# Moving score, inversion and fill work inside a chunked RWKV-7 recurrence

## The chip, the cores and the metric

One core of a Trainium2 chip runs the whole kernel in one launch. PE is the tensor engine, PEld its weight loads, DVE the vector engine, ACT the scalar engine, POOL GpSimd, SP the queue that issues the transfers. The metric is device time in microseconds (us), lower is better; a kernel's time is the median of its runs.

## The reference, cut to what matters

Two layers on 272 tokens (16 learned tokens and 256 of the sequence) of width 2048, all in float32: an RWKV-7 time mixer and an MLP, then gated linear attention and an MLP. The change touches the first mixer only:

```
def step(S, inp):                                   # for each of 32 heads of 64, token after token
    r_t, w_t, k_t, v_t, a_t, b_t = inp
    sa = einsum('bhvk,bhk->bhv', S, a_t)
    S = S * w_t + sa b_t^T + v_t k_t^T
    y = einsum('bhvk,bhk->bhv', S, r_t)
v = xv @ w_rkv[2]                                   # value product
out = ((groupnorm(y) + bonus) * g) @ w_o            # output product
```

## The kernel before

**Products.** Every large product is done as three matmuls of 128x128 weights against 272 tokens, with both operands split into a high and a low part. `wload` (L122) fetches a piece of 128x1024 weights (`raw`, three buffers, SP), rounds it to `hi` on ACT (L132) and subtracts to `lo` on DVE (L133); `hi` and `lo` have two buffers each. A piece serves eight products; `mm3` (L136) is one product, its matmuls have lines L138, L139 and L140. In the recurrence `hi` and `lo` are made in two halves each (`split_parts` = 2).

**The recurrence in chunks.** The 272 tokens are four chunks of 64 and one of 16; the 32 heads are four groups of eight (g = 0 to 3). Within a chunk the recurrence is a small triangular system:

- `scores(g, c)` (L403): PE multiplies keys (`BK`) and receptance and removal vectors (`AR`) of one chunk into two `pt` banks, DVE masks them into `AM` (`AMr` for the short chunk).
- `invert(g)` (L419): DVE alone inverts the triangles of all five chunks of a group. It is a generator of 52 steps: ten transposes into `sysA`, 30 steps of forward substitution (two instructions each, `upd` and `sysA`, each needs the one before it), twelve transposes back (L441 into `t11`, L445 into `AM`). It needs the masks of all chunks.
- `merge(g)` (L518): PE and ACT put the 32-row halves together, in two parts. Its first matmuls have line L530 and need L441's transposes.
- Then for each chunk, in order: `state` (L579: PE on the state `S`, line L587, then DVE `rs`, L590), `solve` (L593: PE L599, ACT `uv`), `emit` (L604: PE L611, DVE adds to and decays `S`, PE L619, ACT `yc`), `turn` (L624: back to `hres`), and `centre` (L548), `keys` (L561), `inner` (L569) for the chunk to come. `state` of a chunk needs `S` from `emit` of the chunk before.
- `norm(g)` (L635): the group norm and the gate, a generator of eight steps; its matmuls are L643 and L652, its DVE lines L647 and L653.

**Fill products.** `products` (L708) is a generator of single products: the value products (256), then the output products of the first twelve of 16 input blocks (192). `R(n)` runs n of them, `until(n)` runs on to the n-th, `some(it, n)` takes n steps of another generator. A value product of group g must be done before group g starts. `split(g)` (L659, ACT and DVE) makes high and low parts of the finished y of a group, which the output products read.

**What sets the order.** In the block from L745 PE's order is the written order. The other engines and the transfers are ordered by a planner at build time, by the order of writing (pieces of weights far ahead of it) and by its own estimate of when each instruction is ready. In group g the kernel runs, for each chunk: `state` and `turn`; a score call of the next group or a few fills; `solve`; `centre`, `keys`; a further score call; fills; `emit`; `inner`. `GAPS` holds the two numbers of fills of each chunk.

The key products (L448 to L478), one for each of 16 blocks f, come before the recurrence; each is 16 products and a string of DVE and ACT work on their result, with two small matmuls (L461, L476). The products write `pj` and `pt` banks in turn, two of each. In them stand the scores of group 0 (after f = 9) and inversion 0 (after f = 13).

## Time and profile before

| what | value |
|---|---|
| median of three runs | 2668.19 us (2666.27 to 2672.52) |
| the profiled execution, its own time | 2671.53 us |
| its span, first to last instruction | 2669.7 us |
| granted PE clock, mean | 0.981 |
| first L530 of merge 0, 1, 2, 3 | 328.2, 410.7, 499.3, 589.9 us |

How to read it: the page gives for each engine its busy time and the number of its instructions. A row of stretches gives begin and end and length, then for each engine its busy time and the count, the granted clock, the share of the DMA engines and GB/s. A row of waits has the engine and line that waited, the one it waited for, total us, times, and the longest. A row in order of time has start, duration, engine, line, operation, tiles written and read, shape and count; in brackets the idle time of the engine before it and who ended it. A row of groups ends with busy us, the mean ns of one, and the idle time before them.

### The profile page before, as it was taken

To read this page: it belongs to the slowest core of one execution; us is meant where nothing else is said; L and a number is where in the kernel's file an instruction comes from. 1 tells how busy PE (TensorE), PEld (TensorE's weight loads), DVE (VectorE), ACT (ScalarE), POOL (GpSimd) and SP (SyncE) were. 2 spreads that over 40 slices of the span, in tenths; PEclk is the share of its full clock that TensorE was granted. 3 is DMA by queue.
4 is the path that set the end of the run, shared out by engine and by line. 5 is a ranking of instruction groups with operands and counts; after the bars stand their busy time and mean duration, and the time that the engine had idled before them with its cause. 6 is when DMAs were issued, how large, how long until landed. Compare 5 with 4: busy or idle time off the path is not lost.

```text
span 2669.7 us, 47686 instructions
## 1 busy us (share of the span) xinstructions
PE 2553.1 (96%) x19492; PEld 2369.1 (89%) x19492; DVE 1687.8 (63%) x2794; ACT 1258.0 (47%) x2011; POOL 10.8 (0%) x35
## 2 busy tenths in 40 slices
PE   7999887779999999999999999999999999999998
PEld 7888886668999999999999999988888888888887
DVE  8678966674755545545545666776766656656665
ACT  5465543435554434434434544454555535435444
POOL 0000000000000000000000000000000000000000
PEclk9999988889999999999999999999999999999999
DMA  5567622213445555545555544444555555555554
GB/s 189 177 226 260 223 92 72 85 58 106 160 166 177 179 174 175 179 176 174 176 179 174 178 152 144 174 150 142 190 184 188 189 190 189 188 187 188 188 189 158
DMA packets 136026, 450.16 MB, mean 169 GB/s; under 512 B 14704, under 2 KB 22640, under 8 KB 135808
## 3 DMA queue, kind: packets, MB, share of 16 engines
q1 hardware_dynamic: 135808, 447.12, 48.4%
q8 instruction: 153, 2.51, 0.4%
q14 instruction: 65, 0.53, 0.1%
HBM read 431.07 MB, written 15.99 MB: 167 GB/s over the span
## 4 chain that ended last, share of the span: by engine, by line
PE 76%; DVE 1%; ACT 0%; issue 0%; DVEq 0%
PE pj L166 23%; PE pj L138 13%; PE pj L140 13%; PE pj L139 13%; PE pj L167 12%; PE pt L899 1%; DVE lo L133 0%; PE pu L908 0%; PE pm L652 0%; PE pt L888 0%; PE pu L910 0%; PE pu L909 0%; PE pm L845 0%; PE pm L643 0%; DVE hres L978 0%; DVE sg L927 0%
## 5 line engine op out<-in xcount | busy, mean ns | idle before, releaser
L133 DVE TENSOR_TENSOR lo<-raw,hi 128x1024 fp32r<-128x1024 f32 (+1 forms) x834 | 946.8, 1142 | 617.4 <-ACT hi L132 603.9
L132 ACT CAST hi<-raw 128x1024 fp32r<-128x1024 f32 (+1 forms) x834 | 813.4, 983 | 1098.5 <-PE pj L139 585.3
L138 PE MATMUL pj<-x,hi 128*128 128x272 f32 x2224 | 661.7, 298 | 6.6 <-ACT x L306 4.1
L140 PE MATMUL pj<-x,lo 128*128 128x272 f32 x2224 | 649.2, 292 | 0.0
L139 PE MATMUL pj<-x,hi 128*128 128x272 f32 x2224 | 647.3, 291 | 0.0
L166 PE MATMUL pj<-x,hi 128*128 128x512 f32 x1664 | 587.9, 397 | 0.6 <-DVE x L818 0.6
L167 PE MATMUL pj<-x,lo 128*128 128x256 f32 x1664 | 469.5, 282 | 1.3 <-DVE lo L133 1.3
L138 PEld LDWEIGHTS pj<-x,hi 128*128 128x128 f32 x2224 | 425.6, 191 | 15.3 <-ACT x L306 4.9
L139 PEld LDWEIGHTS pj<-x,hi 128*128 128x128 f32 x2224 | 428.1, 192 | 2.1
L140 PEld LDWEIGHTS pj<-x,lo 128*128 128x128 f32 x2224 | 424.9, 191 | 0.7
L166 PEld LDWEIGHTS pj<-x,hi 128*128 128x128 f32 x1664 | 313.5, 188 | 76.2 <-issue 2.9
L166 PE MATMUL pj<-h,hi 128*128 128x512 f32 x1024 | 358.5, 395 | 0.0
L167 PEld LDWEIGHTS pj<-x,lo 128*128 128x128 f32 x1664 | 315.0, 189 | 2.9 <-DVE lo L133 1.9
L138 PE MATMUL pj<-h,hi 128*128 128x272 f32 x1024 | 295.3, 288 | 0.0
L140 PE MATMUL pj<-h,lo 128*128 128x272 f32 x1024 | 294.4, 288 | 0.0
L139 PE MATMUL pj<-h,hi 128*128 128x272 f32 x1024 | 294.0, 287 | 0.0
L167 PE MATMUL pj<-h,lo 128*128 128x256 f32 x1024 | 288.9, 282 | 0.0
L166 PEld LDWEIGHTS pj<-h,hi 128*128 128x128 f32 x1024 | 192.7, 188 | 43.6
L167 PEld LDWEIGHTS pj<-h,lo 128*128 128x128 f32 x1024 | 194.3, 190 | 0.0
L139 PEld LDWEIGHTS pj<-h,hi 128*128 128x128 f32 x1024 | 194.1, 190 | 0.0
L138 PEld LDWEIGHTS pj<-h,hi 128*128 128x128 f32 x1024 | 193.2, 189 | 0.0
L140 PEld LDWEIGHTS pj<-h,lo 128*128 128x128 f32 x1024 | 192.4, 188 | 0.0
(246 smaller groups left out, 2213.9 us busy)
## 6 DMA issues: line engine op xcount, KB each, us to landing
raw<-mlp_w_d SPq DMA_DIRECT2D x512, 512.0 KB, 3.2
raw<-gla_in_d SPq DMA_DIRECT2D x98, 512.0 KB, 3.2
raw<-w_rkv_d SPq DMA_DIRECT2D x80, 512.0 KB, 3.4
raw<-gla_o_d SPq DMA_DIRECT2D x32, 512.0 KB, 3.2
raw<-w_r_d SPq DMA_DIRECT2D x16, 512.0 KB, 3.3
raw<-rw_oA_d SPq DMA_DIRECT2D x16, 512.0 KB, 3.2
raw<-rw_oB_d SPq DMA_DIRECT2D x16, 512.0 KB, 3.2
ard<-ar SPq DMA_DIRECT2D x16, 288.0 KB, 3.5
```

The lines of the kernel that those rows point to most:

```text
L132: nc.scalar.copy(hi[:, h], raw[:, h])
L133: nc.vector.tensor_tensor(out=lo[:, h], in0=raw[:, h], in1=hi[:, h].bitcast(F32), op=ALU.subtract)
L138: nc.tensor.matmul(out, hi[:, ws], xh, start=first, stop=False)
L139: nc.tensor.matmul(out, hi[:, ws], xl, start=False, stop=False)
L140: nc.tensor.matmul(out, lo[:, ws], xh, start=False, stop=last)
L166: nc.tensor.matmul(wide, hi[:, ws], x[kt][:, :, off : off + SEQ], start=kt == 0, stop=False)
L167: nc.tensor.matmul(ps[:, :SEQ], lo[:, ws], x[kt][:, 0, off : off + SEQ], start=False, stop=kt == nk - 1)
L899: nc.tensor.matmul(pa[:w, i * C : (i + 1) * C], KX[i][:, dt, s * P : s * P + w], Q[:, dt, i * C : (i + 1) * C], start=dt == 0, stop=dt == 1)
```

## The change

- **Scores.** The five score calls of the next group were one in chunk 0, two in chunk 1 and two in chunk 2; now two in chunk 0 and three in chunk 1. The inversion of the next group is started in chunk 1 instead of chunk 2.
- **Inversion steps.** Portions of nine (twice in each chunk from chunk 1's end on) instead of eight and six; all 52 are written by chunk 4's first portion instead of 36 with the rest behind `until`.
- **Fills.** `GAPS` moves fills from the last chunks to chunk 2 and spreads group 3's evenly. `MARK` replaces the fixed marks: at the merges of groups 1, 2, 3 the fills stand at 134, 214, 286 instead of 120, 184, 248. Around the second half of a merge there are 4, 2 and 4 fills instead of 8, 4 and 3. Groups 0 to 2 take 80, 80 and 72 fills instead of 64 each (the first of them with those that open the next group).
- **Inversion 0** runs in portions of seven in each key product after f = 7; the scores of group 0 come after f = 6 instead of 9, their loads after f = 4 instead of 7.
- **Weight pieces** come from one list (`order`, `srcs`); `ahead` asks for the next piece at the fourth product of the one that is running, instead of at its own first.
- **Norm steps** are taken four in each of chunks 0 and 1, instead of four, three and the rest.
- **Loads.** `AR` of the group after next is fetched in two parts, in chunks 3 and 4, instead of once behind the group; `BK` in chunk 2 as before.
- The last split and the last 64 output products join `order`; they run after `until(448)` and the release of the recurrence's memory, where they stood before.

```
-GAPS = [[(2, 1), (2, 1), (2, 1), (8, 8), (8, 8)],
-        [(2, 1), (2, 1), (2, 1), (8, 8), (8, 8)],
-        [(2, 1), (2, 1), (2, 2), (10, 10), (10, 10)],
-        [(2, 2), (2, 2), (10, 10), (10, 10), (10, 10)]]
+GAPS = [[(2, 1), (2, 1), (8, 8), (9, 9), (9, 9)],
+        [(2, 1), (2, 1), (8, 8), (9, 9), (9, 9)],
+        [(2, 1), (2, 1), (8, 8), (8, 8), (8, 8)],
+        [(4, 4), (4, 4), (4, 4), (4, 4), (4, 4)]]
+MARK = [134, 214, 286]
...
+        def fetch(g, dst, src, a=0, b=576):
+            nc.sync.dma_start(dst[g % 2][:, :, a:b], src[4 * g : 4 * g + 4, :, a:b].rearrange("f p n -> p f n"))
...
-            if f == 7:
+            if f == 4:
                 load(0)
-            if f == 9:
+            if f == 6:
                 for c in range(5):
                     scores(0, c)
-            if f == 13:
-                for _ in invert(0):
-                    pass
+                inv = invert(0)
+            if f > 7:
+                for _ in range(7):
+                    next(inv, None)
...
-                hi, lo = self.wload(s)
+                hi, lo = weights.pop(0)
                 for j in range(8):
+                    if j == 3:
+                        ahead()
...
+        def ahead():
+            if srcs:
+                weights.append(self.wload(srcs.pop(0)))
...
             for g in range(NG):
-                V = 64 * (g + 2) if g < 3 else 0
+                more = g + 1 < NG
                 for c in range(5):
                     if c:
                         state(g, c)
                         turn(g, c - 1)
-                    if g + 1 < NG and c in (1, 2):
-                        scores(g + 1, 2 * c - 1)
-                        R(1)
-                    else:
+                    if more and c < 2:
+                        scores(g + 1, 2 * c)
+                    elif not more:
                         some(last, 1)
-                        R(GAPS[g][c][0])
-                    some(inv, 6)
+                    R(GAPS[g][c][0])
+                    some(inv, 9)
                     solve(g, c)
                     if c in (1, 3):
                         centre(g, c + 1)
                     if c < 3:
                         keys(g, c + 1)
-                    if g + 1 < NG and c < 3:
-                        scores(g + 1, 2 * c)
-                        if c == 2:
-                            inv = invert(g + 1)
-                    some(last, 3)
+                    if more and c < 2:
+                        scores(g + 1, 2 * c + 1)
+                    some(last, 4)
                     R(GAPS[g][c][1])
-                    some(inv, 8)
+                    if more and c == 1:
+                        scores(g + 1, 4)
+                        inv = invert(g + 1)
+                    some(inv, 9)
                     emit(g, c)
                     if c < 4:
                         inner(g, c + 1)
-                    if c == 2 and g + 2 < NG:
-                        load(g + 2, ar=False)
-                some(last, 99)
-                if g + 2 < NG:
-                    load(g + 2, bk=False)
-                if g + 1 < NG:
-                    until(V - 8)
+                    if g + 2 < NG and c == 2:
+                        fetch(g + 2, BKs, bkd)
+                    if g + 2 < NG and c == 3:
+                        fetch(g + 2, ARs, ard, 0, 512)
+                    if g + 2 < NG and c == 4:
+                        fetch(g + 2, ARs, ard, 512)
+                if more:
+                    until(MARK[g])
                     some(inv, 99)
                     m = merge(g + 1)
                     next(m)
-                    until(V)
+                    R(4)
                     turn(g, 4)
-                    R(4)
+                    R(2)
                     next(m)
                     for f in (centre, keys, inner):
                         f(g + 1, 0)
-                    R(3)
+                    R(4)
...
         for _ in last:
             R(4)
-        R(999)
+        until(448)
         win.close()
         wl.close()
-        split(3)
-        for f in range(8):
-            for _ in outB(1, f):
-                pass
+        R(999)
```

More of the change, by code (lines that the diff above doesn't have):

```diff
@@ L396, in put, with load @@
             tt(dst[:, o + skip : o + 16], a[:, 4 * C + skip :], b[:, 4 * C + skip :])
-        def load(g, bk=True, ar=True):
-            for on, dst, src in ((bk, BKs, bkd), (ar, ARs, ard)):
-                if on:
-                    nc.sync.dma_start(dst[g % 2], src[4 * g : 4 * g + 4].rearrange("f p n -> p f n"))
+        def fetch(g, dst, src, a=0, b=576):
+            nc.sync.dma_start(dst[g % 2][:, :, a:b], src[4 * g : 4 * g + 4, :, a:b].rearrange("f p n -> p f n"))
+        def load(g):
+            fetch(g, BKs, bkd)
+            fetch(g, ARs, ard)
         def scores(g, c):
@@ L665, in rwkv, with units @@
         loc = [hres[:, f] if f < 12 else rr[f - 4] for f in range(KT)]
-        def units(x, srcs, ps):
-            for i, s in enumerate(srcs):
-                hi, lo = self.wload(s)
+        def units(x, n, ps):
+            for i in range(n):
+                hi, lo = weights.pop(0)
                 for j in range(8):
+                    if j == 3:
+                        ahead()
                     kt = 8 * i + j
-                    self.mm3(ps, hi, lo, slice(j * P, (j + 1) * P), x[kt][:, 0], x[kt][:, 1], kt == 0,
-                             kt == 8 * len(srcs) - 1)
-                    if kt < 8 * len(srcs) - 1:
+                    self.mm3(ps, hi, lo, slice(j * P, (j + 1) * P), x[kt][:, 0], x[kt][:, 1], kt == 0, kt == 8 * n - 1)
+                    if kt < 8 * n - 1:
                         yield
@@ L679, in v_proj @@
             ps = self.pj()[:, :T]
-            yield from units(xv, pair(wv, f), ps)
+            yield from units(xv, 2, ps)
             nc.scalar.copy(hres[:, f], ps)
@@ L686, in outA @@
             ps = self.pj()[:, :T]
-            yield from units(yo, [ap["rw_oA"][f]], ps)
+            yield from units(yo, 1, ps)
             xin = rr[f % 8] if f < 12 else loc[f]
@@ L693, in outB @@
         def outB(s, fp):
-            hi, lo = self.wload(ap["rw_oB"][s, fp])
+            hi, lo = weights.pop(0)
             pss = [self.pj()[:, :T] for _ in range(2)]
@@ L697, in outB @@
                 for j in range(4):
+                    if (i, j) == (0, 3):
+                        ahead()
                     y = yo[8 + 4 * s + j]
@@ L706, in outB @@
                 yield
-        def products():
-            for f in range(KT):
-                yield from v_proj(f)
-            split(0)
-            split(1)
-            for f in range(8):
-                yield from outA(f)
-            split(2)
-            for f in range(2):
-                yield from outB(0, f)
-            for f in range(8, 12):
-                yield from outA(f)
-            for f in range(2, 6):
-                yield from outB(0, f)
-            for f in range(12, 16):
-                yield from outA(f)
-            for f in range(6, 8):
-                yield from outB(0, f)
+        order = [(v_proj, f) for f in range(KT)] + [(split, 0), (split, 1)] + [(outA, f) for f in range(8)] + [(split, 2)]
+        order += [(outB, 0, 0), (outB, 0, 1)] + [(outA, f) for f in range(8, 12)] + [(outB, 0, f) for f in range(2, 6)]
+        order += [(outA, f) for f in range(12, 16)] + [(outB, 0, 6), (outB, 0, 7), (split, 3)]
+        order += [(outB, 1, f) for f in range(8)]
+        srcs = []
+        for k, *a in order:
+            srcs += pair(wv, a[0]) if k == v_proj else [ap["rw_oA"][a[0]]] if k == outA else [ap["rw_oB"][a[0], a[1]]] if k == outB else []
+        weights = []
+        def ahead():
+            if srcs:
+                weights.append(self.wload(srcs.pop(0)))
+        def products():
+            for k, *a in order:
+                if k == split:
+                    split(*a)
+                else:
+                    yield from k(*a)
         work = products()
@@ L744, in rwkv @@
         load(1)
+        ahead()
         with tc.manual_schedule(engines={mybir.EngineType.PE}):
@@ L804, in rwkv @@
             R(4)
-        R(999)
+        until(448)
         win.close()
         wl.close()
-        split(3)
-        for f in range(8):
-            for _ in outB(1, f):
-                pass
+        R(999)
         self.split_parts = 1
```

## The prediction

> **What bounds the kernel now.** I read the page first, then busy time by stretch, then the waits of PE, then the vector engine (DVE) and PE in order of time inside the recurrence. The page's first lines:

> ```profile
> span 2669.7 us, 47686 instructions
> ## 1 busy us (share of the span) xinstructions
> PE 2553.1 (96%) x19492; PEld 2369.1 (89%) x19492; DVE 1687.8 (63%) x2794; ACT 1258.0 (47%) x2011; POOL 10.8 (0%) x35
> ```

> PE is idle for 2669.7 - 2553.1 = 117 us. The stretches below are, in turn: key products up to score group 0; from there to merge 0; then for each of groups 0 to 2 a front part (merge to the masks of score chunk 3) and a back part (to the next merge); last, group 3. Then come the waits of PE in 320 to 690 us, and the first merge.

> ```profile
> core 0: us, PE busy (x) PEld busy (x) DVE busy (x) ACT busy (x) POOL busy (x), PEclk, DMA share, GB/s
> 196.00:241.00 45.00, 43.39 (x315) 41.03 (x314) 34.06 (x85) 30.02 (x57) 0.00 (x0) 1.00 0.91 304
> 241.00:328.10 87.10, 76.45 (x554) 71.23 (x552) 84.20 (x233) 46.27 (x91) 0.16 (x1) 0.96 0.63 216
> 328.10:363.20 35.10, 33.22 (x530) 29.44 (x530) 11.85 (x22) 14.66 (x34) 1.46 (x2) 0.81 0.17 61
> 363.20:410.60 47.40, 32.27 (x422) 29.84 (x418) 44.65 (x110) 15.86 (x35) 0.16 (x1) 0.85 0.37 128
> 410.60:452.50 41.90, 37.36 (x576) 31.95 (x576) 16.87 (x33) 19.85 (x47) 1.46 (x2) 0.93 0.15 47
> 452.50:499.20 46.70, 29.56 (x403) 26.93 (x401) 44.12 (x108) 14.72 (x33) 0.16 (x1) 0.85 0.36 125
> 499.20:541.10 41.90, 37.38 (x575) 31.99 (x575) 16.82 (x33) 19.85 (x47) 1.46 (x2) 0.93 0.15 46
> 541.10:589.90 48.80, 29.59 (x405) 27.07 (x402) 46.45 (x117) 17.08 (x41) 0.16 (x1) 0.83 0.21 72
> 589.90:678.10 88.20, 83.48 (x1076) 75.75 (x1077) 43.53 (x88) 47.04 (x106) 0.52 (x1) 0.96 0.29 96
> ```

> ```profile
> PE pt L530 <- DVE sysA L441: 47.9, 4, 14.9
> PE pu L587 <- DVE S L266: 12.9, 9, 3.2
> ```

> ```profile
> 328.16 1.92 PE L530 MATMUL pt<-sysA,AM 32*32 32x32 f32 x64 [8.02 <-DVE sysA L441]
> ```

> So fronts are PE's, with DVE 34 to 40% busy; backs are DVE's, 94 to 95% busy, and PE sits out 15 to 19 us of each. What PE waits for is the inversion: 47.9 us at the four merges, 8.02 at merge 0 and so 39.9 at the other three. What DVE does in the stretch from 241 us and in the back of group 0: the inversion (first two rows, the tile sysA), then, by the groups of that back, pieces of weights (`lo`, two halves each); below them, by tile (ns: shortest, median, longest), the small ones that the sums need.

> ```profile
> 241.00:328.10 87.10, 32.19 (x82) 0.96 0.63 216
> 363.20:410.60 47.40, 31.83 (x82) 0.85 0.37 128
> ```

> ```profile
> L133 DVE TENSOR_TENSOR lo<-raw,hi 128x512 fp32r<-128x512 f32 x14 | 9.0, 686 | 0.3 <-ACT hi L132 0.3
> ```

> ```profile
> L266 DVE TENSOR_TENSOR S<-pu,S x2: 425/425/425, 368.3 to 382.4; 128x256 f32<-128x256 f32 x2
> L266 DVE TENSOR_TENSOR S<-S,WC x2: 420/423/426, 369.4 to 383.0; 128x256 f32<-128x256 f32 x2
> ```

> ```profile
> L590 DVE SCALAR_TENSOR_TENSOR rs<-pu,rs x32: 412/418/428, 351.3 to 652.3; 64x256 f32<-64x256 f32 x24, 32x256 f32<-32x256 f32 x8
> ```

> ```profile
> L647 DVE SCALAR_TENSOR_TENSOR ysq<-hres,vecs,ysq x16: 496/501/505, 428.1 to 677.1; 128x272 f32<-128x272 f32 x16
> L266 DVE TENSOR_TENSOR r<-r,ysq x16: 432/441/443, 428.6 to 677.6; 128x272 f32<-128x272 f32 x16
> ```

> **The change, part by part.** No arithmetic is added or removed: PE, ACT and DVE do the same products, so time can only come from waits and from the clock. Fill products are 448 before the last 64 in both; they only change place.

> *Inversion 0 among the key products.* Its 82 DVE instructions (32.2 us), and before them the score masks of group 0, move three to five key products earlier. DVE is full from 241 us until merge 0 (84.2 of 87.1) but has 45.0 - 34.1 = 10.9 us free in 196 to 241. The masks (five pairs, the full ones 1.29 us by the rows at 357.10 and 441.88 below, so about 6 us) go into that room, and inversion steps may follow, so DVE should be through 6 to 9 us earlier. PE lost 8.02 us there. I take 6. Bounds: 0, if the key products' own DVE work, now behind seven steps in each product, holds PE as long; 10, if wait and half clock both go. Price if its cover goes: rival C.

> The clock after such a wait, PE alone in three stretches of 3 us (busy and count, granted clock; the first is a run of fill products in the recurrence, the second follows merge 1, the third an S wait of 2.57 us, whose row stands below):

> ```profile
> 378.40:381.40 3.00, 3.00 (x24) 1.00 0.03 5
> 412.60:415.60 3.00, 3.00 (x13) 0.50 0.01 3
> 461.10:464.10 3.00, 3.00 (x14) 0.50 0.01 3
> ```

> ```profile
> 459.90 0.24 PE L587 MATMUL pu<-S,AR 64*64 64x64 f32 x1 [2.57 <-DVE S L266]
> ```

> A fill product (three matmuls) is 3.00/8 = 0.375 us at full clock, about 0.67 at half. After merge 0, half clock costs 18 matmuls some 2 us. Whether a shortened wait keeps the clock lies between 0 and 2; the third row fell to 0.50 after only 2.6 us, so I take 1. [...]

> *Scores in chunks 0 and 1, the front.* The masks of score chunk 2 in groups 0 and 1 are now, with the PE groups of 416 to 506 us for score calls and norm:

> ```profile
> 357.10 1.29 DVE L266 TENSOR_TENSOR AM<-pt,cst 128x512 f32<-128x512 f32 x2 [2.71 <-PE pt L412]
> ```

> ```profile
> 441.88 1.29 DVE L266 TENSOR_TENSOR AM<-pt,cst 128x512 f32<-128x512 f32 x2 [2.71 <-PE pt L412]
> ```

> ```profile
> L412 PE MATMUL pt<-AR,BK 64*128 64x128 f32 (+1 forms) x80 | 6.3, 275 | 0.1
> L652 PE MATMUL pm<-gs,g 128*128 128x272 f32 x16 | 4.7, 419 | 1.2 <-ACT ysq L644 1.2
> ```

> Score chunk 3 takes the place that chunk 2 has now (masks over at 358.4 and 443.2), plus one more call on PE (6.3/5 = 1.3 us) and one more fill (0.4). Group 0's front then is 358.4 + 1.7 - 328.1 = 32.0 us instead of 35.1. In group 1, fills between merge and first emit go from 8+4+3 to 4+2+4, five fewer (1.9 us, and some 0.6 less at half clock): 443.2 + 1.7 - 2.5 - 410.6 = 31.8, say 32 instead of 41.9, since the second half of the norm and chunk 1's emit move behind the masks. Group 2 the same.

> *The backs.* An inversion is a chain that DVE must end before a merge, so a back lasts what DVE has in it. To 47.4, 46.7 and 48.8 us I add: fills, by GAPS and the marks 65, 65 and 57 (now 50, 43, 43), one piece of weights for eight, 2 x 0.686 with 0.08 of overlap = 1.29: 10.5, 10.5 and 9.2 us against 9.0, 7.7 and 7.7; one value add (0.4); chunk 1's S pair (0.85) and chunk 2's two rs (0.84); in groups 1 and 2 four norm steps more, six DVE operations of 0.44 to 0.50 (the third kind, L653, taken as L647), less one that is there: 2.4. Backs: 47.4+1.5+0.4+1.7 = 51.0; 46.7+2.8+0.4+1.7+2.4 = 54.0; 48.8+1.5+0.4+1.7+2.4 = 54.8.

> PE has less than that to do in them: 32.3 + 15 x 0.375 + 2.5 (emit and inner of chunk 1, 48 short matmul records; at most 3 x 1.3 by the score row) = 40.4; 29.6 + 22 x 0.375 + 2.5 + 4 (half a norm, an estimate from the 4.7) = 44.4; 29.6 + 14 x 0.375 + 2.5 + 4 = 41.4. So merges 1 to 3 still wait, some 6, 8 and 11 us after S waits, instead of 39.9 in all.

> Groups: 83.0, 86.0 and 86.8 us against 82.5, 88.6 and 90.7: 6.0 us shorter, and at merge 3 there are 286 fills done instead of 248: 38 x 0.375 = 14.3 us less to do behind it, where PE is 95% busy (83.48 of 88.20).

> *S waits.* Now the S of the chunk with the first inversion steps waits for eight transposes:

> ```profile
> 366.21 2.07 DVE L427 STREAM_TRANSPOSE sysA<-AM 32x256 f32<-32x256 f32 x4
> 368.31 0.42 DVE L266 TENSOR_TENSOR S<-pu,S 128x256 f32<-128x256 f32 x1
> 368.77 0.60 DVE L430 STREAM_TRANSPOSE sysA<-AMr 32x256 f32<-32x256 f32 x1
> ```

> ```profile
> 369.97 0.34 PE L587 MATMUL pu<-S,AR 64*64 64x64 f32 x1 [3.20 <-DVE S L266]
> ```

> That wait comes one chunk earlier, with nine transposes: 3 to 5 us, inside a back that DVE sets anyway. Later S's slip in between two inversion operations:

> ```profile
> 381.98 0.38 DVE L266 TENSOR_TENSOR sysA<-sysA,upd 128x210 f32<-128x210 f32 x1
> 382.39 0.42 DVE L266 TENSOR_TENSOR S<-pu,S 128x256 f32<-128x256 f32 x1
> ```

> *Costed at nothing.* Weight pieces requested at the fourth product of the one before: `hi` has two buffers, the one asked for is free by then either way, and the list of PE's waits has none on `hi` or `lo` in this stage; without that cover a piece costs 1.29 us of DVE. AR fetched in two parts and sooner on SP: the parts wait for states 3 and 4, the weight loads queue behind them, three `raw` buffers (24 fills, 9 us) cover that. The splits of y for the output products, now at fill 256 inside back 2: eight on DVE there now too. The last eight output products behind `until(448)`: same place. GAPS of 4 in group 3: PE's stage either way.

> *Sum.* 6 + 1 (inversion 0) + 6.0 + 14.3 = 27.3 us. The profiled execution took 2671.53 us (1.8 beside its span); 2671.5 - 27.3 = 2644.2. It is 3.3 above the median of the three runs, which spread over 6 us; I take half of that off: 2643.

> **The rivals.** *B, emitted order on DVE in the groups.* If S of chunks 2 and 3 stands behind all 18 steps emitted before it, a chunk costs DVE 18 of 52 steps, 11 to 13 us of the 32 (the middle ones are the longest), 2.9 of pieces, 2.1 of S, rs and value add, near 18, against PE's 11 to 12: two waits of 6 to 7 us a group, and then 14 us of PE's own (R(9), R(9), until) behind an inversion that has ended. Group 0: 32 + 8 + 18 + 18 + 14 = 90; with 91 and 88 the three are 7 longer than now, not 6 shorter: 2643 + 13 = 2656. For it: the row of the eight transposes; against: the S at 382.39. [...]

> *C, the same order at the key products, the slower side.* DVE has 34.06 us in the 45 us from 196 us, which hold 6 key products (315 matmuls, 52 in each): some 5.6 for a product of 7.4 us; with seven steps (4.3) it needs 9.9. If PE is held for those 2.5 us in each of eight products, before fills can run, merge 0 comes about 10 us later than now instead of 7 earlier; at half clock for 3 us each time (row at 461.10), 12 more. With B: 2656 + 17 + 12 = 2685. It decides from holds of about 2 us in each product and chunk. Against: key products write four PSUM banks in turn, so PE can run ahead, and DVE's work up to merge 0 only moves.

> *D, it moves waits and no more.* Fronts stay as long as now because ACT copies and norms set them, the backs grow: +3.6, +4.9 and +3.6, less 14.3, and inversion 0 gains 0 to 7: 2661 to 2668. For it: PE waits on the norm and on ACT in the fronts (1.2 us in the L652 row); against: those are short, and the front is cut by calls that move out of it.

> *E, all four merge waits go*: 47.9 us, 2621. Against: DVE has 5% free in the backs.

> **How the numbers follow.** Forecast 0.52 (its own range 2632 to 2652), B 0.16, C 0.12, D 0.12, E 0.08. No change is within 0.2%, 5.3 us, of 2668.2. D is mostly inside that: faster 0.78, same 0.10, slower 0.12. The range 2624 to 2666 leaves out C and the outer parts of D and E.

> **What would show it.** Merge 0 waits under 3 us for L441. Masks of score chunk 3 end about 32 us after each merge. Backs of 51 to 55 us with DVE over 93% busy, and merge waits of 5 to 12 us left. S waits of 3 to 5 us, once a group. Wrong if PE's idle time turns up in 200 to 300 us at L461, L476 or L138, if S waits come three times a group, or if the merges wait for nothing.

## The result, and the profile after

The median fell from 2670.01 us (2666.27 to 2672.52, six runs) to 2655.11 us (2648.83 to 2661.69, six runs): ratio 0.9945, interval 0.9928 to 0.9962. The forecast was 2643, the range 2624 to 2666. So the direction was right, and the gain of 14.9 us is about half of the 27.3 in the forecast's sum. The profiled execution took 2651.93 us (span 2649.9, mean clock 0.986). The lines of the code that are named here move by 2 to 5: merge's L530 is now L535, the state's L587 is L592, the score call's L412 is L416, the norm's L643 and L652 are L648 and L657, L441 is L445, `lo` is L135, the fills L140 to L142.

The page of the changed kernel begins:

```profile
span 2649.9 us, 47706 instructions
## 1 busy us (share of the span) xinstructions
PE 2551.9 (96%) x19492; PEld 2364.2 (89%) x19492; DVE 1688.0 (64%) x2794; ACT 1257.3 (47%) x2011; POOL 10.8 (0%) x35
```

PE's idle time is 2649.9 - 2551.9 = 98 us, 19 less than before, and its work is the same. The stretches of before, now: key products up to the score calls of group 0, those calls, the rest up to merge 0; then front and back of groups 0, 1 and 2.

```profile
core 0: us, PE busy (x) PEld busy (x) DVE busy (x) ACT busy (x) POOL busy (x), PEclk, DMA share, GB/s
196.00:218.00 22.00, 21.67 (x158) 20.51 (x158) 18.68 (x49) 15.30 (x30) 0.00 (x0) 1.00 0.87 299
218.00:240.00 22.00, 14.78 (x89) 11.94 (x88) 11.21 (x30) 6.50 (x14) 0.00 (x0) 0.60 0.53 199
240.00:331.80 91.80, 87.07 (x624) 82.44 (x624) 87.68 (x241) 53.42 (x103) 0.16 (x1) 0.98 0.66 216
331.80:357.80 26.00, 23.85 (x421) 21.03 (x420) 10.26 (x19) 12.79 (x30) 0.95 (x1) 1.00 0.41 148
357.80:408.80 51.00, 41.41 (x572) 38.66 (x572) 47.93 (x116) 19.16 (x43) 0.68 (x2) 0.90 0.36 120
408.80:439.90 31.10, 27.53 (x441) 22.86 (x440) 13.47 (x25) 16.93 (x40) 0.95 (x1) 1.00 0.22 71
439.90:494.20 54.30, 46.20 (x587) 41.73 (x588) 49.76 (x120) 20.50 (x46) 0.68 (x2) 0.91 0.36 118
494.20:525.30 31.10, 27.53 (x440) 22.85 (x440) 14.80 (x27) 16.93 (x40) 0.95 (x1) 1.00 0.25 78
525.30:581.80 56.50, 43.01 (x561) 38.55 (x561) 52.24 (x130) 21.45 (x50) 0.68 (x2) 0.90 0.26 83
```

PE's waits in the recurrence, then the first matmul of merges 0, 2 and 3 (merge 1, at 408.78, waits for nothing either):

```profile
PE pu L592 <- DVE S L268: 17.8, 10, 3.3
PE pm L648 <- DVE hres L658: 8.1, 6, 2.4
PE pt L535 <- DVE sysA L445: 6.5, 2, 6.3
PE pm L657 <- ACT ysq L649: 5.9, 10, 0.6
PE pu L592 <- DVE upd L268: 5.0, 1, 5.0
```

```profile
331.81 0.38 PE L535 MATMUL pt<-sysA,AM 32*32 32x32 f32 x12
...
494.18 0.60 PE L535 MATMUL pt<-sysA,AM 32*32 32x32 f32 x27 [0.19 <-DVE sysA L445]
...
581.85 0.58 PE L535 MATMUL pt<-sysA,AM 32*32 32x32 f32 x14 [6.32 <-DVE sysA L445]
```

Three things stand out. The merges wait 6.5 us in all instead of 47.9. Yet the state's waits have grown from 12.9 to 22.8 us (two rows, S and `upd`), and merge 0, which waits for nothing, comes 3.6 us later than before. And there is a new hole at 218 us: 22 us with 14.8 of PE work at a clock of 0.60.

For the comparisons I cut each trace at events that all kernels have: the L465 matmul (L461 before) of key product 3, near 200 us; each merge's first matmul; the last full mask of each front; the first matmul of the next stage (L225; L223 before). What lies outside these cuts was 2122 to 2135 us in thirteen profiles, with no relation to the edits that I can see, so a median holds some us of scatter that the cuts don't.

| kernel | median | ratio to before | to merge 0 | front 0 | back 0 | group 1 | group 2 | merge 3 to L225 | sum |
|---|---|---|---|---|---|---|---|---|---|
| before | 2670.0 | | 129.1 | 35.1 | 47.4 | 88.6 | 90.6 | 153.7 | 544.6 |
| changed | 2655.1 | 0.9945 | 132.6 | 26.0 | 51.0 | 85.4 | 87.7 | 142.4 | 525.0 |
| e0, changed again | 2661.0 | 0.9956 | 132.3 | 30.5 | 52.3 | 86.4 | 87.9 | 144.9 | 534.2 |
| e1 | 2658.5 | 0.9946 | 129.4 | 28.0 | 52.4 | 86.2 | 87.9 | 145.0 | 528.8 |
| e2 | 2669.5 | 0.9998 | 132.4 | 29.4 | 47.1 | 88.3 | 90.5 | 153.6 | 541.3 |
| e3 | 2657.5 | 0.9944 | 123.6 | 32.3 | 51.0 | 85.1 | 87.0 | 146.7 | 525.7 |
| e4 | 2655.7 | 0.9941 | 132.4 | 26.0 | 52.4 | 86.4 | 87.9 | 140.8 | 525.8 |
| e5 | 2655.0 | 0.9942 | 132.8 | 26.0 | 52.1 | 86.4 | 90.2 | 141.6 | 529.0 |
| e6 | 2653.5 | 0.9930 | 131.4 | 27.5 | 49.2 | 85.6 | 88.5 | 142.4 | 524.6 |
| e7 | 2645.5 | 0.9890 | 119.8 | 32.9 | 52.5 | 86.3 | 91.2 | 136.8 | 519.4 |
| e8 | 2650.9 | 0.9928 | 122.2 | 33.4 | 52.1 | 86.2 | 91.2 | 137.2 | 522.2 |
| e9 | 2643.3 | 0.9893 | 120.7 | 32.9 | 52.0 | 82.9 | 87.1 | 138.8 | 514.4 |
| e10 | 2637.2 | 0.9868 | 132.6 | 26.2 | 50.1 | 85.1 | 79.4 | 133.5 | 506.9 |

The intervals of the ratios are 0.001 to 0.0025 wide to each side. Each ratio is to the kernel before as it ran together with that kernel (medians 2670.0 to 2671.3 us), and it is not the quotient of the two medians.

### The profile page after: what moved, and what is told of

It is laid out like the page before. It is cut to its first block, busy times and chain, and to the rows that moved or that the text cites. A ratio compares the mean times of both kernels' runs of the same rounds, so it can differ in the third digit from the quotient of the medians.

```text
span 2649.9 us, 47706 instructions
## 1 busy us (share of the span) xinstructions
PE 2551.9 (96%) x19492; PEld 2364.2 (89%) x19492; DVE 1688.0 (64%) x2794; ACT 1257.3 (47%) x2011; POOL 10.8 (0%) x35
## 4 chain that ended last, share of the span: by engine, by line
PE 77%; DVE 3%; ACT 1%; issue 0%; DVEq 0%; ACTq 0%
PE pj L168 23%; PE pj L140 13%; PE pj L142 13%; PE pj L141 13%; PE pj L169 12%; DVE lo L135 1%; PE pt L908 1%; PE pm L657 0%; PE pu L917 0%; DVE upd L268 0%; PE pt L897 0%; DVE sysA L268 0%; PE pm L648 0%; PE pm L558 0%; PE pt L416 0%
## 5 line engine op out<-in xcount | busy, mean ns | idle before, releaser
L135 DVE TENSOR_TENSOR lo<-raw,hi 128x1024 fp32r<-128x1024 f32 (+1 forms) x834 | 946.8, 1142 | 596.6 <-ACT hi L134 583.6
L140 PE MATMUL pj<-x,hi 128*128 128x272 f32 x2224 | 657.0, 296 | 6.6 <-ACT x L308 4.1
L142 PE MATMUL pj<-x,lo 128*128 128x272 f32 x2224 | 645.1, 290 | 0.2 <-DVE lo L135 0.2
L140 PEld LDWEIGHTS pj<-x,hi 128*128 128x128 f32 x2224 | 421.4, 190 | 15.1 <-ACT x L308 4.9
L142 PEld LDWEIGHTS pj<-x,lo 128*128 128x128 f32 x2224 | 420.7, 189 | 1.6 <-DVE lo L135 0.7
L140 PE MATMUL pj<-h,hi 128*128 128x272 f32 x1024 | 294.7, 288 | 0.0
L142 PE MATMUL pj<-h,lo 128*128 128x272 f32 x1024 | 293.9, 287 | 0.0
L140 PEld LDWEIGHTS pj<-h,hi 128*128 128x128 f32 x1024 | 192.6, 188 | 0.0
L142 PEld LDWEIGHTS pj<-h,lo 128*128 128x128 f32 x1024 | 192.1, 188 | 0.0
```

Source lines behind the costliest of these rows:

```text
L135: nc.vector.tensor_tensor(out=lo[:, h], in0=raw[:, h], in1=hi[:, h].bitcast(F32), op=ALU.subtract)
L140: nc.tensor.matmul(out, hi[:, ws], xh, start=first, stop=False)
L142: nc.tensor.matmul(out, lo[:, ws], xh, start=False, stop=last)
```

## The experiments

**e0, what of a trace repeats.** The changed kernel, unaltered.

> The changed kernel once more, unaltered, to see what of a trace repeats. In the profiles so far the granted clock is half in pieces of 3.4, 6.8, 10.2, 13.7, 17.1 or 20.5 us, and behind the same 6.3 us wait at merge 3 it stayed half for 6.8 us in one program and 20.5 in another. Theory (the clock is granted in steps of about 3.4 us that the program's start doesn't set): waits of PE repeat to within 0.5 us each, but the pieces of half clock don't, and the time from merge 3 to the first L225 differs by 2 to 5 us from the 142.4 us of the first profile. Rival (the clock follows the waits; runs differ only in transfers): the same pieces within one step, 142.4 us within 0.7.

Median 2660.97 us, ratio 0.9956 (0.9939 to 0.9973). The recurrence took 9.2 us longer than in the first profile of the same kernel, more than I expected, 4.5 of it in front 0, where I had expected nothing. The part from merge 3 to L225 was 2.5 us longer, inside the 2 to 5 expected. In front 0 the clock did it: the stretches of 3.4 us from 7 to 8 us behind merge 0, first profile, then e0, and below them the only two waits of e0 over 0.25 us at that place.

```profile
339.80:343.20 3.40, 1.81 (x26) 1.50 (x28) 1.45 (x3) 2.58 (x6) 0.00 (x0) 1.00 0.62 229
343.20:346.60 3.40, 3.40 (x48) 2.89 (x48) 1.29 (x2) 1.33 (x4) 0.00 (x0) 1.00 0.31 106
```

```profile
339.80:343.20 3.40, 2.04 (x16) 1.61 (x14) 1.65 (x3) 2.42 (x5) 0.00 (x0) 1.00 0.76 287
343.20:346.60 3.40, 3.08 (x33) 2.74 (x33) 0.00 (x0) 1.61 (x4) 0.00 (x0) 0.56 0.66 225
346.60:350.00 3.40, 3.40 (x28) 2.99 (x26) 1.29 (x2) 0.63 (x2) 0.00 (x0) 0.50 0.00 0
```

```profile
341.76 0.49 PE L558 MATMUL pm<-cst,hres 128*128 128x128 f32 x2 [0.84 <-ACT hres L687]
...
343.52 0.34 PE L578 MATMUL pm<-uv,AM 64*64 64x64 f32 x2 [0.84 <-ACT uv L564]
```

The same two short waits stand in both executions (in the first profile they end at 340.56 and 342.32 us); in one the clock stays full, in the other it is half for 10.2 us. What differs is where the clock's own steps fall. In each of the thirteen traces all pieces of half clock begin on one grid of 3.41 us, and the offset of that grid from the first instruction differs from execution to execution (0.08 us past a multiple of the step in the trace of before, 0.45 in the first of the changed kernel, 2.26 in e0). Cut on that grid, first profile, then e0:

```profile
338.37:341.78 3.41, 2.27 (x18) 1.84 (x16) 1.64 (x3) 2.20 (x5) 0.00 (x0) 1.00 0.56 216
341.78:345.20 3.42, 2.88 (x45) 2.54 (x47) 1.08 (x2) 1.82 (x4) 0.00 (x0) 1.00 0.68 235
```

```profile
340.18:343.59 3.41, 1.73 (x15) 1.31 (x15) 1.65 (x3) 2.76 (x6) 0.00 (x0) 1.00 0.71 253
343.59:347.01 3.42, 3.42 (x34) 3.08 (x35) 0.37 (x1) 1.24 (x3) 0.00 (x0) 0.50 0.59 211
```

In the first profile a border of the grid splits the second wait, and the two windows have 2.27 and 2.88 us of PE's work; in e0 both waits fall into one window, which has 1.73, and half clock begins at its end. Over all thirteen traces, from 60 us on, half clock followed 141 windows at full clock, 132 of them with under 2.0 us of PE's work; it did not follow 9437, and 58 of these had under 2.0 (in the traces of before and of the changed kernel alone: 22, 21, 1450 and 7).

The waits themselves repeat less exactly than I expected: the state's waits on S are twelve with 20.4 us, against ten with 17.8. So the first profile of the changed kernel was one with little half clock (58.0 us of it in the cuts, 78.5 in e0), and differences of a few us between two traces count only where no piece of half clock lies.

**e1, inversion 0 put back.**

```
-            if f == 4: load(0)
-            if f == 6: ... scores(0, c) ...; inv = invert(0)
-            if f > 7: seven steps of inv
+            if f == 7: load(0)
+            if f == 9: ... scores(0, c) ...
+            if f == 13: the whole of invert(0)
```

> The changed kernel with scores and inversion of group 0 put back where they stood (loads after key product 7, scores after 9, the whole inversion written at 13). Theory (the score block lost in the key products what the inversion gained; what the move brought in the end is the full clock behind merge 0): merge 0 is again near 328 us behind a wait of about 8 us for L445, the front of group 0 lasts 30 to 32 us at a granted clock near 0.8 instead of 26.0 at 1.00, groups 1 to 3 stay as in the changed kernel; 2655 - 3.7 + 6 = about 2657 us. Rival (the move of inversion 0 is a plain loss of 3.7 us): front 26 us, 2651 us.

Median 2658.45 us (ratio 0.9946, 0.9934 to 0.9958), between the two results of the changed kernel. Merge 0 came 3 us earlier in the cuts, behind its wait of 8.03 us; front 0 took 28.0 us, less than I expected. From the first cut to the end of front 0 it is 157.4 us, against 158.6 and 162.8 with the inversion moved. So in this kernel the move is worth nothing that these runs can tell.

**e2, inversion 0 alone.** The kernel before with the lines that e1 takes out.

> The kernel before with nothing but the scores and inversion of group 0 moved forward as in the changed kernel. Theory: PE holds for about 20 us at the five score calls, merge 0 near 332 us without a wait, front of group 0 about 29 us instead of 35.1 because the clock stays full; 2670 + 3.7 - 6 = about 2668 us. Rival (plain loss): front 35, 2674 us. My prediction's step (6 + 1 us gain): 2663 us.

Median 2669.51 us, ratio 0.9998 (0.9989 to 1.0007): no gain, where my prediction's step had 7 us. The theory's pieces are there: merge 0 waits for nothing and is 3.3 us later, front 0 has 29.4 us instead of 35.1, at a granted clock of 1.00 instead of 0.81, the sum of the cuts is 3.3 us shorter.

**e3, the scores of group 0 one key product later.** `if f == 6` becomes `if f == 7`. This asks what the hole at 218 us is. In the changed kernel PE did this:

```profile
220.24 0.73 PE L465 MATMUL pm<-sq,cst 128*128 128x272 f32 x2 [1.86 <-ACT sq L462]
223.78 2.08 PE L416 MATMUL pt<-AR,BK 64*128 64x128 f32 x16 [2.81 <-DMA AR<-ard]
226.61 2.67 PE L416 MATMUL pt<-AR,BK 64*128 64x128 f32 x16 [0.75 <-DVE AM L268]
229.65 2.67 PE L416 MATMUL pt<-AR,BK 64*128 64x128 f32 x16 [0.37 <-DVE AM L268]
233.37 1.22 PE L416 MATMUL pt<-AR,BK 64*128 64x128 f32 x4 [1.05 <-DVE AM L268]
```

> The changed kernel with the scores of group 0 one key product later (after 7 instead of 6); nothing else. Odd key products write the two pt banks, even ones pj; behind product 6 the next one (7) needs a pt bank, and the five score calls take both pt banks each, so no product can run among them; behind product 7 the next one (8) writes pj. Theory (banks): fills run among the score calls, PE's 22 us hold at 218 to 240 us shrinks to about 12 us, merge 0 near 321 to 323 us, still without a wait of over 2 us; 2655 - 10 = about 2645 us. Rival (score calls are slow beside DVE's masks and a late AR load wherever they stand): merge 0 at 328 to 333, 2652 to 2657 us.

```profile
225.16 1.16 PE L416 MATMUL pt<-AR,BK 64*128 64x128 f32 x8
226.25 0.39 PE L140 MATMUL pj<-x,hi 128*128 128x272 f32 x1
226.47 0.29 PE L141 MATMUL pj<-x,hi 128*128 128x272 f32 x1
```

The theory of the banks holds: a key product on `pj` runs among the first score calls (as in the kernel before, where L138 runs at 241.74 us between calls at 240.66 and 242.83), the clock stays full until 243 us (0.96 over 220 to 245 us), and merge 0 comes 9.0 us earlier in the cuts. One part stays unseparated: 2.81 of the hole's 7.2 us without work ended with the transfer of `AR`, and the later place gives that transfer a key product more as well. But the time did not follow: front 0 took 32.3 us instead of 26.0. DVE still had work of the last key products there (15.9 us busy in that front instead of 10.3), L545 waited 2.8 us for ACT's copies, L480 of the last key product ran inside the merge at 325 us behind a wait of 1.0, and 3.4 us of the front ran at half clock. The end of front 0 came 2.7 us earlier than in the first profile, and merge 3 3.6 us. Median 2657.53 us (0.9944, 0.9933 to 0.9956): the 10 us did not come. So most of what PE won there was lost again in front 0.

**e4, group 3.** `GAPS[3]` begins with (8, 4) instead of (4, 4). In the changed kernel, DVE and then PE in group 3 (a chunk's S, and the state that needs it):

```profile
618.57 1.29 DVE L135 TENSOR_TENSOR lo<-raw,hi 128x512 fp32r<-128x512 f32 x2
619.78 0.42 DVE L268 TENSOR_TENSOR S<-pu,S 128x256 f32<-128x256 f32 x1
620.24 0.43 DVE L268 TENSOR_TENSOR S<-S,WC 128x256 f32<-128x256 f32 x1
```

```profile
620.81 0.24 PE L592 MATMUL pu<-S,AR 64*64 64x64 f32 x1 [1.11 <-DVE S L268]
```

> The changed kernel with 8 fills instead of 4 at the first place of group 3, nothing else there: eight fills a chunk are one piece of weights a chunk, and the piece that ends just before emit has its successor's lo (1.29 us) put in front of S on DVE; four fills more shift that point to the place before solve. Theory: the waits of L592 on S in group 3, 4.1 us in four, fall under 1.5 us, and the time from merge 3 to the end falls by 2.5 to 4 us: about 2652 us. Rival (hi and lo now hold uv on ACT and rs on DVE for as long): the waits turn up at L604 or L616, 2655 us.

All four waits (4.1 us) went; in e4 DVE takes S as soon as PE has it:

```profile
628.60 0.42 DVE L268 TENSOR_TENSOR S<-pu,S 128x256 f32<-128x256 f32 x1 [0.40 <-PE pu L616]
```

From merge 3 on e4 took 140.8 us. e0 is the one to compare, with the same 13.7 us of half clock behind merge 3: 144.9 (e1, also with 13.7 us, has 145.0), so 4.1 us. The median, 2655.74 us (0.9941, 0.9923 to 0.9959), does not resolve that.

**e5, more fills in the wait of merge 3.** `MARK = [134, 214, 302]`.

> The changed kernel with MARK 302 instead of 286 at the merge of group 3: 16 fills more in the back of group 2, where PE waits 6.3 us. Theory (that wait is room): the wait at merge 3 falls to 2 to 4 us (two more pieces of 1.29 us on DVE come ahead of L445), merge 3 comes 2 to 3 us later, and 6 us less of fills stand behind it: 3 to 5 us faster, about 2651 us. Rival (DVE is full there, each piece pushes the inversion and half clock stretches the fills): merge 3 comes 6 us later behind the same wait, 2655 us.

Here `split(2)` comes before the norm of group 2 has ended, so the output products read one block of y that is not final; the instructions are the same. The wait fell to 3.5 us and group 2 grew by 2.3 to 2.5 us, the two pieces of the theory. But half clock behind merge 3 lasted 17.1 us, and the part behind it shrank by 0.8 to 3.3 us instead of 6. Median 2655.04 us (2645.01 to 2670.26; 0.9942, 0.9922 to 0.9963): inconclusive, the scatter of the runs is larger than the effect looked for.

**e6, S ahead of the inversion steps.**

```
-                    some(inv, 9)
                     emit(g, c)
+                    some(inv, 9)
```

> The changed kernel with the order of two lines turned: emit is written before the second portion of nine inversion steps of its chunk, instead of behind it. Theory (S waits on DVE behind the portion written ahead of it, and in groups 0 and 1 PE has no slack left, so each such wait counts): the 17.8 us of waits of L592 on S fall under 9 us, merges 1 and 2 come 3 to 5 us earlier in their groups, about 2648 us. Rival (DVE's work in a back is what it is): the S waits go, and the merges wait for L445 by as much, 2655 us. A third outcome: the planner puts the steps where they stood, nothing moves, 2655 us.

In group 0 the first of the three S waits, 5.04 us in the changed kernel, became 1.58, and back 0 took 49.2 us instead of 51.0 and 52.3. The others stayed, and in all the waits on S are 22.8 us, against 22.8 and 25.4 in the two profiles of the changed kernel (with `upd`): a changed place in the order of writing moves only some of the steps on DVE. Median 2653.5 us (0.9930, 0.9912 to 0.9949). The theory held at one wait out of many.

**e7, three edits together** (e3, e4 and e5).

> The changed kernel with three edits together: scores of group 0 after key product 7, eight fills at the first place of group 3, MARK 302. If they add: 3 us (merge 3 came that much earlier with the scores moved) + 1.6 (group 3 without S waits) + 4 = about 2647 us. If they eat one another (DVE's end in each back sets the merges): 2652 us.

Median 2645.53 us, ratio 0.9890 (0.9872 to 0.9909); as in e5, some output products read values that are not final. That is the forecast of adding, though none of the three alone had shown in its median (2657.5, 2655.7 and 2655.0). Merge 3 to L225 took 136.8 us. **e8** has the same aims without that: e3 and `MARK = [134, 214, 298]`, which moves the pieces of group 3 by four fills as well.

> The changed kernel with two edits: the scores of group 0 after key product 7, and MARK 298 at the merge of group 3, which puts 12 fills more into PE's wait there and also moves the end of a piece of weights in group 3 from the place before emit to the place before solve. If the causes found so far are right: 3 us (scores) + 4 us (four S waits of about 1 us in group 3 go) + 0 to 2 us: 2646 to 2650 us, against 2655 to 2661 for the changed kernel. If the gain of the three edits together came from output products being read early rather than from these places: 2655 us.

Median 2650.9 us, ratio 0.9928 (0.9908 to 0.9948): just above the 2646 to 2650, and the interval does not exclude 2655. The cuts are clearer: behind merge 3 it took 137.2 us, as in e7, with no wait on S in group 3 and with the same 13.7 us of half clock as e0, which took 144.9.

**e9, the norm spread out.** On top of e8, in groups 0 to 2:

```
                         scores(g + 1, 2 * c)
+                        some(last, 1)
...
-                    some(last, 4)
+                    some(last, 2 if more else 4)
                     R(GAPS[g][c][1])
+                    if more:
+                        some(last, 1)
```

> The same as e8_best, and in groups 0 to 2 the four norm steps of chunks 0 and 1 are no longer written in one run: one before the first fills, two before the second, one behind them. Theory (the norm's chain PE - ACT - DVE - PE has nothing beside it when four steps stand together: waits of L648 and L657, 14.0 us in all, of which some 10 in groups 1 and 2): those waits halve, 3 to 5 us faster than e8_best. Rival (the time moves to the waits for S and L445, since DVE sets the backs): within 1.5 us of e8_best.

```profile
PE pm L648 <- DVE hres L658: 4.1, 6, 0.9
...
PE pm L657 <- ACT ysq L649: 2.0, 6, 0.6
```

Waits of 14.0 us became 6.1, and groups 1 and 2 shrank by 3.3 and 4.1 us against e8, together more than the 3 to 5 forecast. The waits for S and L445 did not take it up: 20.4 and 4.9 us, against 21.2 and 4.3 in e8. The median is 2643.27 us (2638.58 to 2650.82), ratio 0.9893 (0.9872 to 0.9915). Of the kernels here that leave nothing out it is the fastest.

**e10, what a back lasts.**

```
+                if self.split_parts == 1:
                     nc.vector.tensor_tensor(out=lo[:, h], in0=raw[:, h], in1=hi[:, h].bitcast(F32), op=ALU.subtract)
-        return hi, lo
+        return hi, lo if self.split_parts == 1 else hi
```

> The changed kernel without the low parts of the weights in the recurrence: the subtraction that makes lo is left out there, and the third matmul of a fill reads hi instead; so about eight pieces of 1.29 us, 10 us, go from DVE in each back, and nothing from PE. Theory (the backs last what DVE has in them, waits on S and on L445 are two faces of that): backs shrink from 51 to 57 us to 43 to 48 us, where PE's own 41 to 46 us take over, the waits on S fall by half or more, those of group 3 go; 20 to 30 us faster, 2628 to 2638 us. Rival (PE's chain through ACT and DVE sets the backs): they shrink by under 3 us each, 2645 to 2652 us.

The three backs, and PE's waits on S in all groups:

```profile
358.70:408.90 50.20, 41.04 (x572) 38.28 (x573) 39.81 (x102) 19.17 (x43) 0.68 (x2) 0.93 0.37 122
439.90:494.00 54.10, 46.06 (x585) 41.68 (x585) 42.96 (x107) 20.37 (x46) 0.68 (x2) 0.91 0.38 123
525.00:573.40 48.40, 41.66 (x561) 37.46 (x561) 44.97 (x116) 21.37 (x50) 0.68 (x2) 0.93 0.26 84
```

```profile
PE pu L593 <- DVE S L269: 12.9, 8, 2.9
PE pu L593 <- DVE upd L269: 5.0, 1, 5.0
```

DVE has 7 to 8 us less in each. Backs 0 and 1 did not move (50.2 and 54.1, against 51.0 and 54.3), with DVE now 79% busy; back 2 fell from 56.5 to 48.4, and merge 3's wait is gone. So the theory holds in group 2 and the rival in groups 0 and 1. The waits on S did not fall by half: of the changed kernel's 22.8 us the 4.1 in group 3 are gone, and the 18.7 in groups 0 to 2 are still 17.9. There it is the inversion's own steps that stand ahead of S, not the pieces of weights. Median 2637.17 us (0.9868, 0.9843 to 0.9892), most of the gain in group 2 and behind merge 3, where S waits for no piece. The mean clock of that execution was 0.989, that of e0 0.983.

## Why the prediction was right and wrong, step by step

In the terms of the sum: inversion 0 was to give 6 + 1 us, the groups 6.0, the part behind merge 3 14.3, in all 27.3. In the cuts of the first profile and of e0, the way to merge 0 became 3.5 and 3.2 us longer, the groups 11.7 and 4.7 shorter, the part behind merge 3 11.3 and 8.8 shorter: 19.5 and 10.3 in all. So 2655 lies inside the range partly by luck: a front 0 shorter than forecast made up for a part of what was lost ahead of merge 0. Of the signs named for being wrong, one is rival C's (below), and the two others came in part: merges 1 and 2 wait for nothing, and the state waits for S three times in group 0, in e0 in groups 1 and 2 as well.

**Inversion 0: forecast 7 us, measured none in the time (e2).** DVE was through early, as worked out. The transposes that merge 0 needs, before (L441) and in the changed kernel (L445), with the start of the first and last at the end of the second part:

```profile
L441 DVE STREAM_TRANSPOSE sysA<-sysA x4: 575/575/618, 325.9 to 327.4; 32x256 f32<-32x256 f32 x4
```

```profile
L445 DVE STREAM_TRANSPOSE sysA<-sysA x4: 626/639/680, 315.2 to 318.4; 32x256 f32<-32x256 f32 x4
```

That is 9 us earlier, at the upper end of the "6 to 9 us". The step that failed stands before it: I moved the score calls as work of DVE alone, "The masks ... go into that room", and asked of PE only whether the key products' DVE work would hold it. PE was held, but in the main by banks (e3). A score call takes both `pt` banks; the key product behind product 6 writes `pt`, that behind product 9 wrote `pj`. So for 22 us no product could run between the calls. I had used the four banks as an argument against rival C ("PE can run ahead"); for a block of calls that takes two of them the argument fails. The second failed term is the clock: I put 1 us on it, although the row of that front has a granted clock of 0.81 over 35.1 us, up to 6.7 us, an estimate from that row. Front 0 fell to 26.0 or 30.5 us, 32.0 forecast, and to 29.4 in e2, where only the move of inversion 0 and its scores acts on it. The second miss makes up for a part of the first: some 10 us lost ahead of merge 0, 2 to 6 won behind it.

**Fronts: right.** 31.1 and 31.1 us in groups 1 and 2, 31.8 and 32 forecast.

**Backs: right lengths, wrong reason in two of three.** 51.0, 54.3 and 56.5 us, against 51.0, 54.0 and 54.8. I had DVE set them all and merges 1 to 3 wait 6, 8 and 11 us. They wait 0, 0.2 and 6.3. In groups 0 and 1 PE's own chain is as long, which e10 shows: PE's work in back 0 was sized well (41.4 us at a granted clock of 0.90, 40.4 forecast), but I left out the waits that stand in its chain. In back 0 these three come to 9.5, and 41.4 + 9.5 is the back's 51.0:

```profile
365.26 0.33 PE L592 MATMUL pu<-S,AR 64*64 64x64 f32 x1 [5.04 <-DVE upd L268]
...
378.35 0.24 PE L592 MATMUL pu<-S,AR 64*64 64x64 f32 x1 [1.15 <-DVE S L268]
...
393.24 0.28 PE L592 MATMUL pu<-S,AR 64*32 64x64 f32 x1 [3.34 <-DVE S L268]
```

The step that failed is "3 to 5 us, inside a back that DVE sets anyway", with "once a group". The first wait has the size and place forecast. The later ones were to slip in between two inversion steps, and on DVE they do; but what DVE has just ahead of S is enough for 1 to 3 us, and without any piece of weights it is still so (e10). That is rival B's mechanism at about a third of its price. B as a whole is wrong: groups 0 to 2 did not get 7 us longer.

**Behind merge 3: forecast 14.3 us, measured 11.3 and 8.8.** 38 fills fewer were right. The term costed at nothing, "GAPS of 4 in group 3", costs 4.1 us (e4 against e0): eight fills a chunk are just one piece a chunk, each ends before emit, and its successor's `lo` stands in front of S four times. What is then left of the gap, about 1.4 us in e0, no run isolates; half clock behind merge 3 lasted 7.5 us before, 5.7 in the first profile and 12.9 in e0.

**Costed at nothing, and no wait shows a price:** weight pieces asked for earlier and the AR fetch in two parts, which no run takes out by themselves. No wait of PE on `hi` or AR stands in the recurrence, the only one on `lo`, 0.2 us, is in the key products. The AR wait of 2.81 us at the first score call belongs to the load of group 0.

**The rivals.** C's sign of trouble came true (waits in 200 to 300 us at L465 and L480, 3.5 and 1.7 us) at a small part of its price. D's range began at 2661, where e0's median lies; its reason, fronts that stay long, is wrong. E's merge waits nearly all went, yet its 2621 did not come: PE's idle time fell by 19 us only, since 10 us turned into waits for S and the hole at 218 us has 7 us without work.

Open: why half clock behind merge 3 lasts so unequally behind much the same wait; how much of the hole at 218 us is the late AR; and what makes the time outside the cuts scatter by up to 13 us.

## What to carry to other kernels

Before a block of work moves, look at which buffers it holds and what the next work on the engine writes: here one place more brought merge 0 forward by 9 us, of which 2.7 were left at the end of front 0. When two engines are balanced, a wait inside a chain must be added to the busy time of the engine that waits, not counted as hidden under the other one (back 0: 41.4 us of PE's work and 9.5 of its waits against 51.0). And when fills are spread evenly, check that their count does not fall into step with what comes once per piece: eight fills a chunk put a `lo` in front of each of four S in group 3.

## What the runs showed of the hardware

```profile
574.10:594.60 20.50, 16.57 (x203) 15.39 (x204) 6.05 (x16) 7.85 (x19) 0.00 (x0) 0.50 0.15 52
594.60:598.00 3.40, 3.40 (x36) 3.06 (x35) 2.56 (x5) 2.50 (x7) 0.00 (x0) 1.00 0.22 52
```

Between two executions of the changed kernel it goes with most of 9 us (525.0 and 534.2 us in the table, with 20.5 us more of half clock in the second and 2.6 us more of waits for S).
